# A decoder trunk in one kernel: earlier key loads, later output stores, and deeper query buffers in the last stage

## The chip, the core and the metric

The kernel runs on one core of a Trainium2 chip. Its engines are TensorE (PE, matrix products and transposes), VectorE (DVE), ScalarE (ACT), GpSimd (POOL), and SyncE (SP), whose queue issues the transfers (DMAs) between the chip's main memory and the on-chip buffer. Each engine works through its own list of instructions in the order in which they were put at build time; between engines they wait on semaphores. The metric is the device time of one execution in microseconds (us), the median over runs.

## The reference

One sequence of 2048 rows of width 1024, all in float32, goes through two layers:

```
layer A:  h = rms_norm(x)*(1+scale)+shift;  u,v,z = split(h @ w_in)
          y = gelu(u) * (causal_128x128_mix(rms_norm(gelu(v))) + b) * silu(z)
          x = x + gate * (y @ w_out)
keys:     k,v = split(rms_mod(x) @ w_kv);   k = rms_norm(k)    (3 groups x 2 heads of 128)
layer B:  q,z = split(rms_mod(x) @ w_in);   q = rms_norm(q)/sqrt(128)   (3 groups x 8 heads)
          for group g with dilation d in (1, 4, 16):
              each block of 128 (dilated) rows looks at its own and the previous block
              s = q k^T - slope*distance;  m = max s;  p = exp(s-m);  l = sum p
              o_g = p v / l;   lse_g = m + log l
          o = sum_g softmax_g(lse) * o_g;   out = x + gate * ((o * silu(z)) @ w_out)
```

The modulation (scale, shift, gate) comes from small products of a conditioning vector.

## The kernel before, in words

The 2048 rows are 16 tiles of 128, in four quarters. Each quarter passes through layer A, the key and value product, and the query and `z` products (`dense_s`, line 306, products of sums of blocks: `pd_z3ba` and its like); weights are loaded as `raw_*`, split in two halves by ACT (L260) and DVE (L262), and the matmuls are done in threes, as high x high, low x high and high x low. Queries, keys, `z` and attention outputs travel through main memory (`qd`, `kvd`, `zd`, `od`).

Attention works in units (g, b, kh): group, block of 128 queries, one of two key heads with its four query heads. A unit has four steps, of which a different one is done at each turn of `attend`. `att_1` takes the key block `kv` and the query block `qt` from main memory, transposes both on PE (`pk` L1362, `pq` L1374) and copies them back (`kT`, and `qT` by ACT L1379 and DVE L1380). `att_2` computes the scores (`ps` L1407 to L1409, twelve matmuls 128x256), adds the distance bias on DVE (L1413), takes the maximum (L1416, L1417) and the exponential on ACT (L1423). `att_3` transposes the weights (`pp` L1465, copied to `pT`), `att_4` multiplies with the values (`po` L1484), and stores `ot` to `od` (L1491). Four units are under way at once. The query of the next unit, and with the first of two heads its keys, are loaded in one go ahead of `att_1`. `qt` has two buffers, `kv` four (the tag `xin`), and eight buffers with the tag `st`, made by `sum_tile`, hold sums in the query and `z` products.

`attend` is a generator, run a step at a time between the matmuls of other stages: `tick` counts matmul groups and runs the generators in `fillers` at the rate `rate[0]`. Group 2 of all blocks runs beside the last quarter's products. Groups 1 and 0 of a quarter run as a filler of the following work (`attend_local`); for the last quarter this is the last stage, the output projection. For each tile t and half n of 512 columns it loads the residual rows (`xr`, L1666), issues the stores that were put off (`flush`, at L1667), runs 24 matmuls (`pf`, L1678 to L1680, with `wo`, and the transposed rows `yb` made by `make_yb`, L1638 to L1641), prepares tile t+2 from the three groups' outputs `og` and `z` (`prepare`: ACT L1613, DVE L1541, L1617, L1618), adds the residual (`of`, L1685) and puts its store off to the next `flush`.

What sets the order: the code runs once at build time, and a scheduler then puts each engine's instructions in a fixed order of its own from what depends on what, so that a change in one place can reorder others. Nearly all DMAs of the kernel are issued on SP, in order. Eight semaphores serve them in turn, so that a DMA on SP also waits for the landing of the eighth DMA before it.

Of the kernel before, what the change touches and what calls it, by code (L numbers as in the profile page):

```python
# [12 lines left out]
F32 = mybir.dt.float32  # L13
# [5 lines left out]
P = 128  # L19
# [3 lines left out]
NQ = 4  # L23
# [11 lines left out]
def trunk(ctx, tc, out, x, c, a_ada_w, a_ada_b, a_norm_g, a_w_in, a_sgu_g, a_w_spatial,  # L35
          a_b_spatial, a_w_out, kv_ada_w, kv_ada_b, kv_norm_g, w_kv, k_norm_g, b_ada_w,
          b_ada_b, b_norm_g, b_w_in, b_q_norm_g, b_w_out, dbg=None):
    nc = tc.nc
# [13 lines left out]
    bp = ctx.enter_context(tc.tile_pool(name="bp", bufs=2))  # L52
    sp = ctx.enter_context(tc.tile_pool(name="sp", bufs=4))
    tp = ctx.enter_context(tc.tile_pool(name="tp", bufs=8))
    ap_ = ctx.enter_context(tc.tile_pool(name="ap", bufs=2))
# [6 lines left out]
    od = [dp.tile([S, D], F32, name=f"od{g}") for g in range(3)]  # L62
# [14 lines left out]
    def fill(n):  # L77

        for _ in range(n):
            if not fillers:  # L80
                return
            g = fillers.pop(0)
            try:
                next(g)
                fillers.append(g)
            except StopIteration:
                pass
# [3 lines left out]
    def tick(part=1.0):  # L91
        rate[1] += rate[0] * part
        n = int(rate[1])
        rate[1] -= n
        fill(n)

    def drain():
        while fillers:
            fill(1)

    def evt(name, dt=F32):
        return ep.tile([P, 512], dt, tag="ev", name=name)

    def pst(name, tag="a"):
        return ps.tile([P, 512], F32, tag=tag, name=name)
# [145 lines left out]
    def flush():  # L251
        jobs = pending[:]
        pending.clear()
        with tc.issue_after(last_ld[0].ins):
            for out_, src in jobs:
                nc.sync.dma_start(out_, src)
# [252 lines left out]
    def sum_tile(nm):  # L509
        return tp.tile([P, 516], F32, tag="st", name=f"st_{nm}")  # L510
# [792 lines left out]
    def blk_rows(t, g, b):  # L1303

        if g == 0:
            return t[b * P:(b + 1) * P]
        if g == 1:
            n, r = divmod(b, 4)
            v = t.rearrange("(n i r) w -> n r i w", n=4, r=4) if len(t.shape) == 2 else \
                t.rearrange("(n i r) g w -> n r i g w", n=4, r=4)  # L1310
            return v[n, r]
        v = t.rearrange("(i r) w -> r i w", r=16) if len(t.shape) == 2 else \
            t.rearrange("(i r) g w -> r i g w", r=16)
        return v[b]
# [8 lines left out]
    def geom(g, b):  # L1323
        prev = None if g == 2 or (g == 0 and b == 0) or (g == 1 and b < 4) else b - (1, 4)[g]
        nk = 1 if prev is None else 2
        return prev, nk, 4 // nk

    def att_kv(g, b, ring):
        prev, nk, _ = geom(g, b)
        kv = xp.tile([P, 2, 512], F32, tag="xin", name=f"kv{g}_{b}")  # L1330
        if prev is not None:
            v, src = (t.rearrange("p (h two d) -> p h two d", h=2, two=2)
                      for t in (kv[:, 0, :], blk_rows(kvd, g, prev)[:, g, :]))
            if ring:
                nc.sync.dma_start(v[:, :, 1, :], src[:, :, 1, :])
            else:
                nc.sync.dma_start(v, src)
        nc.sync.dma_start(kv[:, nk - 1, :], blk_rows(kvd, g, b)[:, g, :])
        return kv.rearrange("p b (h two d) -> p b h two d", h=2, two=2)

    def att_q(g, b, kh):
        qt = ap_.tile([P, 516], F32, tag="qt", name=f"qt{g}_{b}_{kh}")
        nc.sync.dma_start(qt[:, 0:516], blk_rows(qd[g], g, b)[:, kh, 0:516])
        return qt

# [124 lines left out]
    def att_4(u):  # L1470

        g, b, kh = u["id"]
        _, nk, hp = geom(g, b)
        if g == 0:
            k4 = slice(kh * 4, kh * 4 + 4)
            l4 = slice(8 + kh * 4, 12 + kh * 4)
            e1, l1, l0 = stat[1][:, b, k4], stat[1][:, b, l4], stat[0][:, b, l4]
            scale_heads(nc.vector, u["o1"], u["o1"], e1)
            nc.vector.tensor_tensor(l1, l1, e1, ALU.mult)
            nc.vector.tensor_tensor(l0, l0, l1, ALU.add)  # L1480
        po = pst(f"po{g}_{b}_{kh}")
        for h in range(4):
            for j in range(nk):
                nc.tensor.matmul(po[:, h * P:(h + 1) * P], u["pT"][h // hp][:, h % hp, j, :],  # L1484
                                 u["kv"][:, j, kh, 1, :], start=j == 0, stop=j == nk - 1)
        ot = evt(f"ot{g}_{b}_{kh}")
        if g == 0:
            nc.vector.tensor_tensor(ot, po, u["o1"], ALU.add)
        else:
            evac_copy(ot, po)  # L1490
        nc.sync.dma_start(blk_rows(od[g], g, b)[:, kh * 512:(kh + 1) * 512], ot)  # L1491

    def attend_local(Q, wrap=False):

        bs = range(4 * Q, 4 * Q + 4)
        yield from attend([(1, b) for b in bs], wrap)
        v = stat[1][:, 4 * Q:4 * Q + 4, :]
        nc.sync.dma_start(std[1].rearrange("(n i r) c -> i n r c", n=4, r=4)[:, Q], v)
        yield
        nc.sync.dma_start(v, std[1].rearrange("(b i) c -> i b c", i=P)[:, 4 * Q:4 * Q + 4])  # L1500
        yield from attend([(0, b) for b in bs], wrap, 3)

    def attend(blocks, wrap=False, lead=0, skew=1):


        us = [{"id": (g, b, kh), "wrap": wrap and geom(g, b)[1] == 2}
              for g, b in blocks for kh in range(2)]
        for u in us:
            g, b, _ = u["id"]
            nk = geom(g, b)[1]  # L1510
            u["own"] = b % 2 if g == 0 and nk == 2 else nk - 1
            u["ring"] = g == 0 and nk == 2 and (0, b - 1) in blocks and geom(0, b - 1)[1] == 2

        def load(i):
            if i < len(us):
                g, b, kh = us[i]["id"]
                if kh == 0:
                    us[i]["kv"] = us[i + 1]["kv"] = att_kv(g, b, us[i]["ring"])
                us[i]["qt"] = att_q(g, b, kh)

        load(0)
        for _ in range(lead):
            yield
        for i in range(len(us) + 2 + skew):
            for k, st in ((2 + skew, att_4), (1 + skew, att_3), (1, att_2), (0, att_1)):
                if 0 <= i - k < len(us):
                    if k == 0:
                        load(i + 1)
                        if i % 2:
                            us[i]["kT"] = us[i - 1]["kT"]  # L1530
                        elif us[i]["ring"]:
                            us[i]["ring"] = us[i - 1]["kT"]
                    st(us[i - k])
                if i >= k:
                    yield


    def scale_heads(e, out, t, f):

        n = f.shape[-1]  # L1540
        e.tensor_tensor(out.rearrange("p (h d) -> p h d", d=P), t.rearrange("p (h d) -> p h d", d=P),  # L1541
                        f.unsqueeze(2).broadcast_to([P, n, P]), ALU.mult)
# [3 lines left out]
    def finish():  # L1546
# [80 lines left out]
            ys[0] = prepare(0, ogs[0])  # L1627

        def last():
            yield from attend_local(NQ - 1)  # L1630
            yield from weights(NT - TPQ, NT)

        def make_yb(t):
# [26 lines left out]
        for t in range(NT):  # L1660
            rw = slice(t * P, (t + 1) * P)
            yb = ybs[t]
            for n in range(2):
                ns = slice(n * 512, (n + 1) * 512)
                xr = evt(f"xr1{t}_{n}")
                last_ld[0] = nc.sync.dma_start(xr, x1d[rw, ns])  # L1666
                flush()  # L1667
                pt = pst(f"pf{t}_{n}", "d")
                wh, wl = wo[n]
                if n and t + 1 < NT:  # L1670
                    make_yb(t + 1)
                    if t + 3 == NT - TPQ:
                        drain()
                        ogs.update({i: load(i) for i in (t + 3, t + 4)})
                elif n == 0 and t + 4 < NT and t + 4 not in (NT - TPQ, NT - TPQ + 1):
                    ogs[t + 4] = load(t + 4)
                for k in range(KT):
                    nc.tensor.matmul(pt, yb[:, 0, k, :], wh[:, k, :], start=k == 0, stop=False)  # L1678
                    nc.tensor.matmul(pt, yb[:, 0, k, :], wl[:, k, :], start=False, stop=False)  # L1679
                    nc.tensor.matmul(pt, yb[:, 1, k, :], wh[:, k, :], start=False, stop=k == KT - 1)  # L1680
                    tick(0.125)
                    if k % 4 == 2 and t + 2 < NT:
                        ys[t + 2] = prepare(t + 2, ogs[t + 2], 2 * n + k // 4)
                o_ = evt(f"of{t}_{n}")
                nc.vector.tensor_tensor(o_, pt, xr, ALU.add)  # L1685
                pending.append((out[rw, ns], o_))

# [72 lines left out]
```

## Time and profile before

| | |
|---|---|
| median of 3 runs | 2903.24 us (2902.45 to 2907.31) |
| profiled execution | 2904.99 us, its span 2903.3 us |
| PE busy | 2875.6 us of the span |
| DVE, ACT, POOL busy | 2219.1, 1667.6, 258.2 us |
| mean granted clock of TensorE | 0.999 |
| DMA | 239 GB/s over the span |

A profile's busy time is an engine's own; "idle before" is the time in which it stood ahead of an instruction, with what ended that. The granted clock is given as a share of 2.4 GHz: 1.00 is 2.4, 0.50 is 1.2. A span is measured inside an execution, from its first instruction to its last; the execution's own time is some 1.7 us longer.

### The profile page before, as it was taken

What the parts mean: (1) busy time and instruction counts of PE and PEld (TensorE: products, weight loads), DVE (VectorE), ACT (ScalarE), POOL (GpSimd) and SP (SyncE); (2) the same over time, 40 slices, a digit from 0 to 9 for tenths busy, and PEclk for the clock granted to TensorE, in tenths of its full rate; (3) what the DMA queues carried; (4) which work ended last, traced back from release to release, by engine and by line L of the source; (5) the groups of instructions that cost most, each with busy time, mean ns of one, the idle gap of its engine ahead of it and who ended that gap; (6) DMA issues with size and microseconds to landing.
All of it is one profiled execution on the core that took longest, in us unless ns stands there. A gap on an engine that the chain in (4) does not pass through costs nothing. (4 is left out here: it accounts for less than half of the span.)

```text
span 2903.3 us, 44921 instructions
## 1 busy us (share of the span) xinstructions
PE 2875.6 (99%) x14610; PEld 2419.2 (83%) x14610; DVE 2219.1 (76%) x4246; ACT 1667.6 (57%) x3400; POOL 258.2 (9%) x549
## 2 busy tenths in 40 slices
PE   8999999999999999999999999999999999999999
PEld 5888888888888888888888888888888888988887
DVE  6786677787758986887878876987678876888972
ACT  4423345668456765676555665676355667876540
POOL 1000001101011000000010000000010003311100
PEclk9999999999999999999999999999999999999999
DMA  7899788777998577776676676766554667889842
GB/s 258 298 311 297 265 287 292 241 250 249 311 334 284 171 259 225 239 247 201 212 262 198 192 253 212 243 225 197 172 174 155 223 219 238 269 265 340 260 144 87
DMA packets 390783, 693.82 MB, mean 239 GB/s; under 512 B 42027, under 2 KB 119821, under 8 KB 390549
## 3 DMA queue, kind: packets, MB, share of 16 engines
q1 hardware_dynamic: 390548, 690.97, 72.3%
q8 instruction: 115, 1.88, 0.3%
q14 instruction: 120, 0.98, 0.1%
HBM read 530.97 MB, written 159.85 MB: 238 GB/s over the span
## 5 line engine op out<-in xcount | busy, mean ns | idle before, releaser
L306 PE MATMUL pd_kv<-w_kv,hkh 128*128 128x512 f32 x768 | 238.5, 391 | 0.3 <-DMA w_kv<-wk 0.2
L355 PE MATMUL pd_u<-hAh,w_u 128*128 128x512 f32 x512 | 207.8, 406 | 0.0
L355 PE MATMUL pd_z<-hAh,w_z 128*128 128x512 f32 x512 | 205.8, 402 | 0.0
L1423 ACT ACTIVATE pr<-pr,stat,rt 128x256 f32<-128x256 f32 (+1 forms) x320 | 177.4, 556 | 45.3 <-DVE stat L1420 30.0
L357 PE MATMUL pd_u<-hAh,w_u 128*128 128x512 f32 x512 | 200.6, 392 | 1.7 <-DVE w_u L262 1.7
L357 PE MATMUL pd_z<-hAh,w_z 128*128 128x512 f32 x512 | 200.4, 392 | 0.0
L356 PE MATMUL pd_u<-hAl,w_u 128*128 128x512 f32 x512 | 200.0, 391 | 0.0
L356 PE MATMUL pd_z<-hAl,w_z 128*128 128x512 f32 x512 | 199.8, 390 | 0.0
L306 PEld LDWEIGHTS pd_kv<-w_kv,hkh 128*128 128x128 f32 x768 | 143.3, 188 | 30.1 <-ACT w_kv L260 0.6
L1484 PEld LDWEIGHTS po<-kv,pT 128*128 128x128 f32 x1200 | 147.6, 191 | 7.4 <-ACT pT L1321 1.2
L1484 PE MATMUL po<-kv,pT 128*128 128x128 f32 x1200 | 149.8, 275 | 1.0 <-ACT pT L1321 1.0
L306 PE MATMUL pd_kv<-w_kv,hkl 128*128 128x512 f32 x384 | 149.8, 390 | 0.0
L1351 POOL TENSOR_SCALAR rt<-qt 128x4 f32<-128x4 f32 x96 | 26.8, 279 | 1311.9 <-DMA qt<-qd 724.7
L1413 DVE SCALAR_TENSOR_TENSOR pr<-dist,rt,ps 128x256 f32<-128x256 f32 (+1 forms) x320 | 124.7, 431 | 22.4 <-PE ps L1409 10.4
L260 ACT ACTIVATE w_u<-raw_u 128x512 fp32r<-128x512 f32 x96 | 59.5, 628 | 142.4 <-PE pd_u L357 95.2
L260 ACT ACTIVATE w_o<-raw_o 128x512 fp32r<-128x512 f32 x104 | 64.2, 628 | 96.4 <-PE pd_o L306 37.8
L260 ACT ACTIVATE w_q<-raw_q 128x512 fp32r<-128x512 f32 x144 | 88.6, 628 | 49.9 <-PE pd_kv L306 9.9
L357 PEld LDWEIGHTS pd_u<-hAh,w_u 128*128 128x128 f32 x512 | 96.1, 188 | 23.9 <-DVE w_u L262 2.9
L357 PEld LDWEIGHTS pd_z<-hAh,w_z 128*128 128x128 f32 x512 | 96.1, 188 | 21.0
L355 PEld LDWEIGHTS pd_u<-hAh,w_u 128*128 128x128 f32 x512 | 96.5, 188 | 18.4 <-issue 1.7
L356 PEld LDWEIGHTS pd_z<-hAl,w_z 128*128 128x128 f32 x512 | 96.5, 188 | 17.6
L355 PEld LDWEIGHTS pd_z<-hAh,w_z 128*128 128x128 f32 x512 | 96.4, 188 | 17.4
(866 smaller groups left out, 7944.8 us busy)
## 6 DMA issues: line engine op xcount, KB each, us to landing
raw_q<-in_b_w_in_dram SPq DMA_DIRECT2D x144, 256.0 KB, 3.8
w_z<-wuz SPq DMA_DIRECT2D x64, 512.0 KB, 4.3
raw_o<-in_a_w_out_dram SPq DMA_DIRECT2D x104, 256.0 KB, 3.5
qt<-qd SPq DMA_DIRECT2D x96, 258.0 KB, 3.6
raw_v<-in_a_w_in_dram SPq DMA_DIRECT2D x96, 256.0 KB, 4.0
raw_u<-in_a_w_in_dram SPq DMA_DIRECT2D x96, 256.0 KB, 5.3
od<-ot SPq DMA_DIRECT2D x96, 256.0 KB, 2.5
raw_kv<-in_w_kv_dram SPq DMA_DIRECT2D x76, 256.0 KB, 4.7
```

The costliest lines, as they stand in the source:

```text
L260: nc.scalar.activation(hi, src, AF.Copy)
L306: last_mm[0] = nc.tensor.matmul(pt, a, u[:, w, :], start=f, stop=e, skip_group_check=more)
L355: nc.tensor.matmul(pts[i], wh, hh[:, k, :], start=k == 0, stop=False)
L356: nc.tensor.matmul(pts[i], wh, hl[:, k, :], start=False, stop=False)
L357: nc.tensor.matmul(pts[i], wl, hh[:, k, :], start=False, stop=k == KT - 1)
L1351: nc.gpsimd.tensor_scalar(rt[:, 12:16], u["qt"][:, 512:516], 1.0 / P, EPS, ALU.mult, ALU.add)
L1413: nc.vector.scalar_tensor_tensor(pr[:, i, :], dist3[:, d0:d0 + w], u["rt"][:, h:h + 1], psc[:, i, :], ALU.mult, ALU.add)
L1423: nc.scalar.activation(pr[:, i, :], pr[:, i, :], AF.Exp, bias=mneg[:, i:i + 1], scale=u["rt"][:, h:h + 1], accum_out=lsum[:, i:i + 1])
L1484: nc.tensor.matmul(po[:, h * P:(h + 1) * P], u["pT"][h // hp][:, h % hp, j, :], u["kv"][:, j, kh, 1, :], start=j == 0, stop=j == nk - 1)
```

## The change

Three parts. In all attention, the loads of keys and queries are apart: keys are loaded a unit ahead of before, and the stores of `ot`, kept in the list `stores`, are issued at the start of the next step in place of the end of their own. With `deep=True`, which only the last quarter's `attend_local` sets, `qt` is taken from the eight `st` buffers (`sum_tile`), and loaded two units ahead. In the last stage, `flush` stands behind the fourth of eight matmul triples (k == 3) rather than ahead of the first, and `of` goes to the two buffers of the tag `bc`.

```diff
--- before.py
+++ after.py
@@ -1338,8 +1338,9 @@
         nc.sync.dma_start(kv[:, nk - 1, :], blk_rows(kvd, g, b)[:, g, :])
         return kv.rearrange("p b (h two d) -> p b h two d", h=2, two=2)
 
-    def att_q(g, b, kh):
-        qt = ap_.tile([P, 516], F32, tag="qt", name=f"qt{g}_{b}_{kh}")
+    def att_q(g, b, kh, deep):
+        nm = f"qt{g}_{b}_{kh}"
+        qt = sum_tile(nm) if deep else ap_.tile([P, 516], F32, tag="qt", name=nm)
         nc.sync.dma_start(qt[:, 0:516], blk_rows(qd[g], g, b)[:, kh, 0:516])
         return qt
 
@@ -1488,22 +1489,23 @@
             nc.vector.tensor_tensor(ot, po, u["o1"], ALU.add)
         else:
             evac_copy(ot, po)
-        nc.sync.dma_start(blk_rows(od[g], g, b)[:, kh * 512:(kh + 1) * 512], ot)
-
-    def attend_local(Q, wrap=False):
+        u["stores"].append((blk_rows(od[g], g, b)[:, kh * 512:(kh + 1) * 512], ot))
+
+    def attend_local(Q, wrap=False, deep=False):
 
         bs = range(4 * Q, 4 * Q + 4)
-        yield from attend([(1, b) for b in bs], wrap)
+        yield from attend([(1, b) for b in bs], wrap, deep=deep)
         v = stat[1][:, 4 * Q:4 * Q + 4, :]
         nc.sync.dma_start(std[1].rearrange("(n i r) c -> i n r c", n=4, r=4)[:, Q], v)
         yield
         nc.sync.dma_start(v, std[1].rearrange("(b i) c -> i b c", i=P)[:, 4 * Q:4 * Q + 4])
-        yield from attend([(0, b) for b in bs], wrap, 3)
-
-    def attend(blocks, wrap=False, lead=0, skew=1):
-
-
-        us = [{"id": (g, b, kh), "wrap": wrap and geom(g, b)[1] == 2}
+        yield from attend([(0, b) for b in bs], wrap, 3, deep=deep)
+
+    def attend(blocks, wrap=False, lead=0, skew=1, deep=False):
+
+
+        stores = []
+        us = [{"id": (g, b, kh), "wrap": wrap and geom(g, b)[1] == 2, "stores": stores}
               for g, b in blocks for kh in range(2)]
         for u in us:
             g, b, _ = u["id"]
@@ -1511,21 +1513,34 @@
             u["own"] = b % 2 if g == 0 and nk == 2 else nk - 1
             u["ring"] = g == 0 and nk == 2 and (0, b - 1) in blocks and geom(0, b - 1)[1] == 2
 
-        def load(i):
+        def load_kv(i):
             if i < len(us):
-                g, b, kh = us[i]["id"]
-                if kh == 0:
-                    us[i]["kv"] = us[i + 1]["kv"] = att_kv(g, b, us[i]["ring"])
-                us[i]["qt"] = att_q(g, b, kh)
-
-        load(0)
+                g, b, _ = us[i]["id"]
+                us[i]["kv"] = us[i + 1]["kv"] = att_kv(g, b, us[i]["ring"])
+
+        def load_q(i):
+            if i < len(us):
+                us[i]["qt"] = att_q(*us[i]["id"], deep)
+
+        def store():
+            for dst, t in stores:
+                nc.sync.dma_start(dst, t)
+            stores.clear()
+
+        load_kv(0)
+        load_q(0)
+        if deep:
+            load_q(1)
         for _ in range(lead):
             yield
         for i in range(len(us) + 2 + skew):
             for k, st in ((2 + skew, att_4), (1 + skew, att_3), (1, att_2), (0, att_1)):
                 if 0 <= i - k < len(us):
+                    store()
                     if k == 0:
-                        load(i + 1)
+                        load_q(i + 1 + deep)
+                        if i % 2 == skew - 1:
+                            load_kv(i + 3 - skew)
                         if i % 2:
                             us[i]["kT"] = us[i - 1]["kT"]
                         elif us[i]["ring"]:
@@ -1533,6 +1548,7 @@
                     st(us[i - k])
                 if i >= k:
                     yield
+        store()
 
 
     def scale_heads(e, out, t, f):
@@ -1627,7 +1643,7 @@
             ys[0] = prepare(0, ogs[0])
 
         def last():
-            yield from attend_local(NQ - 1)
+            yield from attend_local(NQ - 1, deep=True)
             yield from weights(NT - TPQ, NT)
 
         def make_yb(t):
@@ -1664,7 +1680,6 @@
                 ns = slice(n * 512, (n + 1) * 512)
                 xr = evt(f"xr1{t}_{n}")
                 last_ld[0] = nc.sync.dma_start(xr, x1d[rw, ns])
-                flush()
                 pt = pst(f"pf{t}_{n}", "d")
                 wh, wl = wo[n]
                 if n and t + 1 < NT:
@@ -1679,9 +1694,11 @@
                     nc.tensor.matmul(pt, yb[:, 0, k, :], wl[:, k, :], start=False, stop=False)
                     nc.tensor.matmul(pt, yb[:, 1, k, :], wh[:, k, :], start=False, stop=k == KT - 1)
                     tick(0.125)
+                    if k == 3:
+                        flush()
                     if k % 4 == 2 and t + 2 < NT:
                         ys[t + 2] = prepare(t + 2, ogs[t + 2], 2 * n + k // 4)
-                o_ = evt(f"of{t}_{n}")
+                o_ = bp.tile([P, 512], F32, tag="bc", name=f"of{t}_{n}")
                 nc.vector.tensor_tensor(o_, pt, xr, ALU.add)
                 pending.append((out[rw, ns], o_))
 
```

The work on each engine stays as it was. What moves on PE is the last stage, above all its start. Ahead of this piece stand, in both kernels, the last `pd_z3bb` products, `pyb0`, `pk1_12` and two `pf0_0`. Here is PE of before, from the transposes of the query of unit (1,12,0) on (`pq1_12_0`); `pf0_0` and `pf0_1` are the two halves of tile 0 of the output projection, `ps1_12_00` the unit's first scores:

```order
L1374 MATMUL pq1_12_0_26328<-ident_136,qt1_12_0_26311 128x128
L1680 MATMUL pf0_0_26296<-wo00_25081,yb0_26233 128x512
L1374 MATMUL pq1_12_0_26328<-ident_136,qt1_12_0_26311 128x128 x3
L1678 MATMUL pf0_0_26296<-wo00_25081,yb0_26233 128x512
L1679 MATMUL pf0_0_26296<-wo01_25086,yb0_26233 128x512
L1680 MATMUL pf0_0_26296<-wo00_25081,yb0_26233 128x512
L1678 MATMUL pf0_0_26296<-wo00_25081,yb0_26233 128x512
L1679 MATMUL pf0_0_26296<-wo01_25086,yb0_26233 128x512
L1680 MATMUL pf0_0_26296<-wo00_25081,yb0_26233 128x512
L306 MATMUL pd_z3ba0_25841<-w_z3b22_0_26187,hob33_21805 128x512
L306 MATMUL pd_z3ba1_25842<-w_z3b22_0_26187,hob33_21805 128x512
L1407 MATMUL ps1_12_00_26342<-kT1_12_26325,qT1_12_0_26333 128x256
```

In the changed kernel the same transposes stand at the end of all of tile 0's matmuls and of the products `pd_z3ba`, and the scores right behind them:

```order
L1693 MATMUL pf0_1_26458<-wo10_25997,yb0_26233 128x512
L1694 MATMUL pf0_1_26458<-wo11_26122,yb0_26233 128x512
L1695 MATMUL pf0_1_26458<-wo10_25997,yb0_26233 128x512
L1375 MATMUL pq1_12_0_26331<-ident_136,st_qt1_12_0_26309 128x128 x4
L1408 MATMUL ps1_12_00_26345<-kT1_12_26328,qT1_12_0_26336 128x256
L1409 MATMUL ps1_12_00_26345<-kT1_12_26328,qT1_12_0_26336 128x256
L1408 MATMUL ps1_12_01_26359<-kT1_12_26328,qT1_12_0_26336 128x256
L1409 MATMUL ps1_12_01_26359<-kT1_12_26328,qT1_12_0_26336 128x256
L1410 MATMUL ps1_12_00_26345<-kT1_12_26328,qT1_12_0_26336 128x256
L1408 MATMUL ps1_12_00_26345<-kT1_12_26328,qT1_12_0_26336 128x256
L1409 MATMUL ps1_12_00_26345<-kT1_12_26328,qT1_12_0_26336 128x256
L1410 MATMUL ps1_12_00_26345<-kT1_12_26328,qT1_12_0_26336 128x256
```

Between `pq1_12_0` and its scores no other matmul is left. Somewhat later on PE, before, the weights' transposes of the unit (`pp1_12_00`, `pp1_12_01`) stand among the last matmuls of `pf0_1`:

```order
L1678 MATMUL pf0_1_26457<-wo10_25997,yb0_26233 128x512
L1465 MATMUL pp1_12_00_26399<-ident_136,pr1_12_00_26343 128x128 x2
L1679 MATMUL pf0_1_26457<-wo11_26122,yb0_26233 128x512
L1680 MATMUL pf0_1_26457<-wo10_25997,yb0_26233 128x512
L1465 MATMUL pp1_12_00_26399<-ident_136,pr1_12_00_26343 128x128 x2
L1678 MATMUL pf0_1_26457<-wo10_25997,yb0_26233 128x512
L1679 MATMUL pf0_1_26457<-wo11_26122,yb0_26233 128x512
L1465 MATMUL pp1_12_01_26406<-ident_136,pr1_12_01_26357 128x128 x2
L1407 MATMUL ps1_12_10_26424<-kT1_12_26325,qT1_12_1_26390 128x256
L1408 MATMUL ps1_12_10_26424<-kT1_12_26325,qT1_12_1_26390 128x256
L1465 MATMUL pp1_12_01_26406<-ident_136,pr1_12_01_26357 128x128 x2
```

In the changed kernel the same transposes come right behind the unit's scores and the next query's transposes, and are followed by that query's scores:

```order
L1375 MATMUL pq1_12_1_26385<-ident_136,st_qt1_12_1_26311 128x128 x4
L1466 MATMUL pp1_12_00_26401<-ident_136,pr1_12_00_26346 128x128 x4
L1466 MATMUL pp1_12_01_26408<-ident_136,pr1_12_01_26360 128x128 x2
L1408 MATMUL ps1_12_10_26426<-kT1_12_26328,qT1_12_1_26390 128x256
L1466 MATMUL pp1_12_01_26408<-ident_136,pr1_12_01_26360 128x128 x2
L1409 MATMUL ps1_12_10_26426<-kT1_12_26328,qT1_12_1_26390 128x256
```

All `pf0_1` matmuls have been done by then. On SP, before, the loads of these two queries stand among weights of the third quarter's query product (`raw_q30t4`):

```order
L267 DMA raw_q30t4_0_25734<-wt0_3_106 128x512
L1343 DMA qt1_12_0_26311<-qd1_93 128x516
L267 DMA raw_q30t4_1_25739<-wt0_3_106 128x512
L267 DMA raw_q30t4_2_25744<-wt0_3_106 128x512
L1491 DMA od2_97<-ot2_13_1_25495 128x512
L1343 DMA qt1_12_1_26313<-qd1_93 128x516
```

In the changed kernel they stand behind the loads for tiles 3 and 4 of the output projection:

```order
L1614 DMA og3_0_26284<-od0_95 128x1024
L1614 DMA og3_2_26286<-od2_97 128x1024
L1621 DMA zt3_0_26288<-zd_101 128x512
L1621 DMA zt3_1_26289<-zd_101 128x512
L1682 DMA xr10_0_26292<-x1d_90 128x512
L1614 DMA og4_0_26295<-od0_95 128x1024
L1614 DMA og4_2_26297<-od2_97 128x1024
L1621 DMA zt4_0_26299<-zd_101 128x512
L1621 DMA zt4_1_26300<-zd_101 128x512
L1344 DMA st_qt1_12_0_26309<-qd1_93 128x516
L1344 DMA st_qt1_12_1_26311<-qd1_93 128x516
L1344 DMA st_qt1_13_0_26313<-qd1_93 128x516
```

They have moved by some eighty rows on SP, and are now the first of four queries in a row (the fourth is `qt1_13_1`). The keys of this block, `kv1_12`, stand well ahead of them in both kernels.

## Rows read from the trace of the kernel before

**Rows 1.** The page's first part: busy us of each engine, share of the span, instructions.

```profile
PE 2875.6 (99%) x14610; PEld 2419.2 (83%) x14610; DVE 2219.1 (76%) x4246; ACT 1667.6 (57%) x3400; POOL 258.2 (9%) x549
```

**Rows 2.** PE's waits: engine, line <- what ended the wait: us in all, times, longest.

```profile
PE pva L126 <- DMA veca<-in_a_ada_b_dram: 5.0, 1, 5.0
...
PE pd_o1a L306 <- DVE w_o L262: 1.8, 2, 1.6
PE pd_u L357 <- DVE w_u L262: 1.7, 2, 1.0
PE pp L1465 <- ACT pr L1423: 1.6, 1, 1.6
PE pf L1680 <- DVE yb L1641: 1.4, 1, 1.4
...
PE pd_v10a L306 <- DVE w_v L262: 1.0, 2, 0.8
```

**Rows 3.** Waits of SP's DMA queue, same columns.

```profile
SPq L1343 <- PE pq L1374: 137.9, 67, 6.9
...
SPq L256 <- DVE of L1685: 95.0, 28, 5.5
```

**Rows 4.** PE's timeline, start of last stage: start us, us, line, what, shape, count.

```profile
2619.28 5.61 PE L306 MATMUL pd_z3bb<-w_z3bt,hob 128*128 128x512 f32 x24
...
2626.80 0.27 PE L1374 MATMUL pq<-ident,qt 128*128 128x128 f32 x1
...
2630.41 5.18 PE L306 MATMUL pd_z3ba<-w_z3b,hob 128*128 128x512 f32 x22
...
2644.47 0.38 PE L1465 MATMUL pp<-ident,pr 128*128 128x128 f32 x2
...
2651.77 0.50 PE L1680 MATMUL pf<-wo,yb 128*128 128x512 f32 x1 [1.41 <-DVE yb L1641]
```

**Rows 5.** SP's timeline: DMA issues around the last stage's start.

```profile
2557.89 0.32 SPq L1343 DMA_DIRECT2D qt<-qd  x1
...
2633.58 1.00 SPq L1598 DMA_DIRECT2D og<-od  x2
2634.92 0.99 SPq L1605 DMA_DIRECT2D zt<-zd  x2
...
2644.05 0.32 SPq L1343 DMA_DIRECT2D qt<-qd  x1
```

**Rows 6.** DMA issues from 2620 to 2655 us: count, KB each, median us to landing.

```profile
og<-od SPq DMA_DIRECT2D x9, 512.0 KB, 6.3
zt<-zd SPq DMA_DIRECT2D x8, 256.0 KB, 7.7
...
qt<-qd SPq DMA_DIRECT2D x3, 258.0 KB, 3.2
```

**Rows 7.** ACT's timeline, first unit of group 1.

```profile
2627.67 0.69 ACT L1379 ACTIVATE qT<-pq,gqk 128x512 fp32r<-128x512 f32 x1
...
2642.24 1.28 ACT L1423 ACT_TABLE_LOAD   x1 [1.55 <-DVE stat L1417]
2643.53 0.60 ACT L1423 ACTIVATE pr<-pr,stat,rt 128x256 f32<-128x256 f32 x1
```

**Rows 8.** DVE's timeline, the same unit.

```profile
2628.39 0.75 DVE L1380 SCALAR_TENSOR_TENSOR qT<-pq,gqk,qT 128x512 fp32r<-128x512 f32 x1
...
2639.85 1.26 DVE L1413 SCALAR_TENSOR_TENSOR pr<-dist,rt,ps 128x256 f32<-128x256 f32 x3
...
2642.01 0.15 DVE L1417 SCALAR_TENSOR_TENSOR stat<-rt 128x2 f32<-128x2 f32 x1
```

**Rows 9.** Stretches: us, busy us (count) of PE, PEld, DVE, ACT, POOL, granted clock, DMA, GB/s.

```profile
22.00:24.00 2.00, 1.91 (x3) 0.87 (x4) 1.93 (x4) 0.30 (x1) 0.00 (x0) 0.50 1.05 368
26.00:28.00 2.00, 2.00 (x4) 0.73 (x4) 1.88 (x3) 0.00 (x0) 0.00 (x0) 0.66 1.10 349
2650.00:2652.00 2.00, 0.59 (x3) 0.24 (x2) 2.00 (x5) 2.00 (x8) 1.20 (x2) 1.00 0.34 123
```

## Prediction

> **What bounds the kernel now.** I read the page's busy shares first: TensorE (PE) is busy 2875.6 us, 99% of the span [rows 1]. So a microsecond that any other engine, or a transfer, saves is worth nothing unless PE waits for it, and a microsecond in which PE newly waits goes to the end in full: nothing later has slack to win it back. The second view was the list of PE's waits. With a span of 2903.3 us, PE idles 27.7 us in all. The largest item is the start, before any work (5.0 us for the first vector), and the waits in the body are few and small: 1.8 us for `w_o`, 1.7 for `w_u`, 1.6 for the softmax (`pp`), 1.4 for `yb`, 1.0 for `w_v` [rows 2]. No PE wait in this list is put down to `qt`, `kv`, `od` or `xr`, the transfers that the change moves. They are held up on SP's queue, it is true: the query loads stood 137.9 us behind the last use of their buffer, the output stores 95.0 us behind their sum [rows 3]. But these are waits of a queue that PE doesn't feel. So there is little to win, at most 7.5 us of the body's waits in rows 2, and only as far as late loads cause them. What matters is whether the new order lays bare something that PE's other work covers today.
>
> The third view was PE's timeline where the last stage begins. There unit (1,12,0), the first of the last quarter's group 1, passes through PE beside tile 0 of the output projection. Its `pq` transposes stand at 2626.80, and the first `pp`, which needs its softmax, at 2644.47; the 17.7 us between hold 22 matmuls `pd_z3ba` in a row (5.18 us) and nearly all of tile 0's `pf` [rows 4]. ScalarE (ACT), VectorE (DVE) and this unit's chain have all that time. Its query was asked for at 2557.89, 69 us before use [rows 5].
>
> **The change, part by part.** Keys a unit earlier, stores a step later: the count of loads, stores and arithmetic is the same. On PE the order of the first 7,260 rows or so (everything before the last stage) is unchanged. What can move there is when a weight arrives, behind fewer held issues on SP. The waits of that kind are 1.8 + 1.7 + 1.0 = 4.5 us [rows 2]; they end with DVE's half of the weight split, which has other reasons to be late than SP. I take a third of them, −1.5 us. Bounds: −5 (all of them, and a little more), and +2 (a key load moved in front of a weight makes another wait of the size of the longest in rows 2).
>
> Deep query buffers: the load of `qt1_12_0` goes from among the `raw_q30t4` weights to a place behind `og3`, `zt3`, `xr10_0`, `og4` and `zt4`. SP issues in order, and a DMA goes out only when the eighth before it has landed: `qt1_13_0` at 2644.05 is the eighth behind the second `zt3` issue, about 2635.5, so 8.5 us later, though nothing in its own data held it [rows 5]. The new eighth before `qt1_12_0` is `og3_2`, issued about 2634.3 [rows 5]. An `og` load took 6.3 us here, a `zt` load 7.7, a `qt` load at the end of this busy stretch 3.2 [rows 6]. So the query is issued between 2640.6 and 2642.8, and lands after another 3.2 to 8.5: between 2643.8 and 2651.3. The stretch is full of half-megabyte loads, so I take issue at 2642.1 and 7.0 us, 2649.1.
>
> When does PE want it? In the new order 70 matmuls 128x512 (24 of `pd_z3ba`, of which 22 are the row at 2630.41, and tile 0's 48 `pf`, less the two that stand ahead of `pq` in both) come before `pq1_12_0`. One costs at most 5.61/24 = 0.23 us [rows 4], so 16.1, and PE is there at 2626.80 + 16.1 = 2642.9. Term A, the wait for the query: 2649.1 − 2642.9 = 6.2 us, bounds 0.9 and 8.4. In before it is 0.
>
> Term B, the bare softmax chain. In the new order `pq`, twelve scores, the second `pq`, and the `pp` of the same unit follow each other with no other matmul between. From the landing: `pq` 0.6 (two `pp` transposes took 0.38 [rows 4], four under twice that); `qT` on ACT then DVE, 2627.67 to 2629.14, 1.5 [rows 7, 8]; twelve scores of half a 512 width, 1.4, of which some 0.5 lie beside DVE's part; DVE's bias, maximum and statistics 2639.85 to 2642.16, 2.3 [rows 8]; a table load of 1.28 that starts only when the statistics are there, and four exponentials of 0.6 [rows 7]. Together 0.6 + 1.5 + 0.9 + 2.3 + 1.3 + 2.4 = 9.0 until the last `pp` can start. PE's own work within is 0.6 + 1.4 + 0.6 + 0.5 = 3.1. That would leave 5.9; DVE starts on the first scores before the last are there, so I take 5.5, bounds 4.2 (the table load is out of the way) and 6.5 (`of0_1`, which waits for its late `xr`, now stands between the two statistics on DVE).
>
> Term C: `pf` waited 1.4 us for `yb` in tile 1 [rows 2, 4]. Less work stands between `ps1_12_1` and its `pp` now (four `pf` in place of fourteen), and `yb` has the same two copies ahead, so I change one wait against another of its size: 0, bounds −1.4 and +1.5. Rows from mid tile and `of` in the `bc` buffers touch SP and DVE only: 0, hidden by the `pf` matmuls; without that cover one 128x512 sum, no more than 0.7.
>
> Term D: the clock. With A and B, PE does about 3 us of work in some 15. Early in the kernel, behind the small products of its start, the granted clock was 0.50 at 22 to 24 us (1.2 GHz in place of 2.4), and 0.66 over 26 to 28, on its way back; after the 1.4 us wait for `yb` it was still 1.00 [rows 9]. If the clock falls here it costs as there: 22 to 26 at 0.5 loses 2.0 us and 26 to 28 another 0.7, 2.7 us. The Trainium skill, "TensorE: Matmul & The Clock Gate", Part 1 (The HAM clock gate), says it the other way round: "the default state is throttled, and activity releases the throttle", a rule that speaks against any order with a bare wait. The slow stretch of rows 9 agrees with it; no run here shows yet what a 6 us wait in the body does. By the rule D is 2.7, without it 0. I take 2.7, since two long waits lie close together; bounds 0 and 5.4, if it falls twice.
>
> **Sum.** A 6.2 + B 5.5 + C 0 + D 2.7 − 1.5 = +12.9 us. The profiled execution took 2904.99 us (span 2903.3 and 1.7 around it), 1.75 above the median of the runs, 2903.24. So 2904.99 + 12.9 = 2917.9 for one like it, and 2916.1 for the median. All low ends together give 0.9 + 4.2 − 1.4 + 0 − 5 = −1.3, 2901.9; all high ends 8.4 + 6.5 + 1.5 + 5.4 + 2 = +23.8, 2927.0.
>
> **The rivals.** *The clock holds.* A and B come as above, D is 0: +10.2, 2913.4. For it: the 1.00 after a 1.4 us wait. Against: that wait was a quarter of A.
>
> *The query arrives in time.* SP, no longer behind the `zd` stores and `pq` releases, issues `og3` and `og4` sooner and the query lands as fast as the 3.2 us row: A 0.9, B 4.2, D 0, C 0, −1.5: +3.6, 2906.8, within the noise. For it: SP's queue does lose its long holds [rows 3]. Against: the eighth-DMA rule of rows 5 is not about such holds, and the stretch moves as many bytes as before.
>
> *Faster.* The relief on SP decides: from the point where weights, `yb` and `pp` inputs arrive a microsecond or two sooner throughout, the 7.5 us of rows 2 in the body go, with some 3 us of smaller ones like them, while the query comes in time (A 0) and B is 4.2: −6.3, 2896.9. Against: PE's order leaves B bare whatever SP does, and those waits end with DVE or ACT, none with a load.
>
> *Worse.* Each of the next units stands as bare as the first, since the fillers were spent on tile 0. A second wait of B's size and a longer slow clock: 12.9 + 5.5 + 1.5 = +19.9, 2923.1. For it: `pp1_12_1` has only four `pf` ahead. Against: from the third unit on, `pf` matmuls stand between the steps again.
>
> **How the numbers follow.** Forecast with the clock low 0.40, clock holds 0.27, in time 0.16, faster 0.08, worse 0.09. The range 2903 to 2922 leaves out about 0.10 below and 0.09 above. The likeliest case alone, with its bounds narrowed to one wait of each kind, is 2911 to 2921. About 0.2% (5.8 us) is what a measurement of this kernel can tell from no change: faster than 2897.4 has 0.08, slower than 2909.0 has the first two, the worst, and a little less for their low ends: 0.75; between them 0.17.
>
> **What would show it.** In the profile after: a PE wait at `pq` for the DMA `qt` of 5 to 8 us, near the 16th us of the last stage; right behind it waits at `ps` for `qT` and at `pp` for `pr` that sum to 4 to 6.5; a granted clock near 0.5 in some of the next 5 us; and up to there a PE timeline within 2 us of before. The prediction is wrong if PE's idle time in the last stage doesn't grow by more than 5 us, or if PE's waits for the weights fall by more than 4.

## The result, and the profile after

The changed kernel took 2924.14 us in the median of six runs (2920.27 to 2928.05), the kernel before 2906.72 beside it: a ratio of 1.0065, 95% interval 1.0052 to 1.0078, or 15 to 23 us slower. A second timing on another chip (experiment e6) gave 1.0059 (1.0047 to 1.0071). The forecast was +12.9 us, 2916.1, with a range up to 2922: the right sign and the right place, too small a loss. Of the miss of 8 us, 3.5 is the three runs of before on which it stood, whose median was 2903.24. Four executions of the experiments below took 4,858 to 11,926 us and are left out of the ratios; the traces of e7 and e14 are of two of them and are not used.

The page of the changed kernel, its first part, and its list of PE's waits (cut to what differs; columns as in [rows 1] and [rows 2]):

```profile
PE 2882.4 (99%) x14610; PEld 2423.4 (83%) x14610; DVE 2221.7 (76%) x4246; ACT 1669.1 (57%) x3400; POOL 261.0 (9%) x549
```
```profile
PE pq L1375 <- DMA st_qt<-qd: 5.7, 1, 5.7
...
PE pp L1466 <- ACT pr L1424: 4.4, 4, 2.8
PE pd_u L355 <- ACT w_u L260: 2.2, 1, 2.2
...
PE pq L1375 <- DVE pr L1414: 1.7, 1, 1.7
```

In a span of 2920.5 us PE idles 38.1, in place of 27.7, and is busy for 6.8 us more with the same instructions. The largest new wait is the forecast one, `pq` for the query, 5.7 us; the longest wait of `pp`, 2.8 us, and one of 0.8 at `ps` belong to the bare softmax chain; the wait for `yb` of [rows 2] is gone. A wait of `pd_u` for ACT's copy of a weight, 2.2 us, was not forecast.

PE's timeline in the last stage answers to [rows 4] (start, us, line, what, count):

```profile
2631.23 5.17 PE L306 MATMUL pd_z3ba<-w_z3b,hob 128*128 128x512 f32 x22
...
2644.40 0.39 PE L1695 MATMUL pf<-wo,yb 128*128 128x512 f32 x1
2650.51 1.09 PE L1375 MATMUL pq<-ident,st_qt 128*128 128x128 f32 x4 [5.72 <-DMA st_qt<-qd]
2652.38 0.58 PE L1408 MATMUL ps<-kT,qT 128*128 128x256 f32 x1 [0.78 <-ACT qT L1380]
...
2659.00 1.85 PE L1466 MATMUL pp<-ident,pr 128*128 128x128 f32 x6 [2.84 <-ACT pr L1424]
...
2660.86 0.63 PE L1466 MATMUL pp<-ident,pr 128*128 128x128 f32 x2
...
2664.91 0.60 PE L1363 MATMUL pk<-ident,kv 128*128 128x128 f32 x4
```

The 22 `pd_z3ba` are there as before; then `pf` runs without a break, the last from 2644.40; then PE stands for the query until 2650.51, for `qT`, and for `pr`. The two kernels' way over the same work, from the first `pyb0` to `pk1_13`, before and after, and stretches of the changed kernel (columns as in [rows 9]; the sixth number behind the engines is the granted clock):

```profile
2624.73:2648.83 24.10, 23.84 (x134) 20.00 (x133) 19.95 (x37) 18.44 (x45) 0.00 (x0) 1.00 1.04 401
```
```profile
2626.07:2664.91 38.84, 29.20 (x133) 23.96 (x132) 30.02 (x52) 23.74 (x63) 8.58 (x16) 0.78 1.04 400
2646.00:2648.00 2.00, 0.00 (x0) 0.00 (x0) 2.00 (x4) 0.83 (x3) 0.00 (x0) 0.84 1.03 393
2648.00:2656.00 8.00, 4.71 (x20) 4.10 (x20) 6.52 (x13) 2.30 (x7) 4.85 (x8) 0.50 1.05 402
2656.00:2664.00 8.00, 5.16 (x23) 4.42 (x23) 5.01 (x12) 7.23 (x19) 3.74 (x8) 0.50 1.04 397
2664.00:2666.00 2.00, 2.00 (x15) 1.86 (x14) 2.00 (x6) 1.33 (x3) 0.00 (x0) 0.89 0.85 322
```

24.10 us have become 38.84, 14.7 more: 9.4 of idle time, and 5.4 because the same matmuls run at half clock from 2647 to 2664. Of the span's 17.2 us, 1.3 lie ahead of this stretch and 1.1 behind it.

SP's timeline answers to [rows 5]:

```profile
2634.39 1.00 SPq L1614 DMA_DIRECT2D og<-od  x2
2635.96 1.00 SPq L1621 DMA_DIRECT2D zt<-zd  x2
2637.87 0.32 SPq L1682 DMA_DIRECT2D xr<-x1d  x1
2639.20 0.99 SPq L1614 DMA_DIRECT2D og<-od  x2
2640.55 2.47 SPq L1621 DMA_DIRECT2D zt<-zd  x2
2643.77 2.34 SPq L1344 DMA_DIRECT2D st_qt<-qd  x4
```

The first of the four queries goes out at 2643.77, some 8.7 us behind the `og` that is its eighth before (the second of the pair of 2634.39, sent at 2635.1). It was used 6.7 us later. The forecast said 2642.1 and 7.0 us, in a trace that came to this place 1.3 us sooner.

### The profile page after: what moved, and what is told of

It reads as the page before. It is cut to its first block, busy times and chain, and to the rows that moved or that the text cites. A ratio compares the mean times of both kernels' runs of the same rounds, so it can differ in the third digit from the quotient of the medians.

```text
span 2920.5 us, 44920 instructions
## 1 busy us (share of the span) xinstructions
PE 2882.4 (99%) x14610; PEld 2423.4 (83%) x14610; DVE 2221.7 (76%) x4246; ACT 1669.1 (57%) x3400; POOL 261.0 (9%) x549
## 5 line engine op out<-in xcount | busy, mean ns | idle before, releaser
L260 ACT ACTIVATE w_u<-raw_u 128x512 fp32r<-128x512 f32 x96 | 59.7, 628 | 139.9 <-PE pd_u L357 92.1
L260 ACT ACTIVATE w_o<-raw_o 128x512 fp32r<-128x512 f32 x104 | 64.3, 628 | 95.2 <-PE pd_o L306 37.6
L260 ACT ACTIVATE w_q<-raw_q 128x512 fp32r<-128x512 f32 x144 | 88.9, 628 | 50.9 <-PE pd_kv L306 9.9
L355 PEld LDWEIGHTS pd_z<-hAh,w_z 128*128 128x128 f32 x512 | 96.4, 188 | 17.4
```

The lines of the kernel that those rows point to most:

```text
L260: nc.scalar.activation(hi, src, AF.Copy)
L355: nc.tensor.matmul(pts[i], wh, hh[:, k, :], start=k == 0, stop=False)
```

## The experiments

Theory 1 was the forecast's: the late place of the first query's load, brought by the deep buffers, is the loss. All ratios are against the kernel before on the same chip, with a 95% interval.

**e1, keys and stores.** Edit to the changed kernel (this and the next three; `...` marks lines left out, and the `flush()` put in stands ahead of the tile's matmuls, as before):

```diff
-            yield from attend_local(NQ - 1, deep=True)
+            yield from attend_local(NQ - 1)
...
+                flush()
...
-                    if k == 3:
-                        flush()
...
-                o_ = bp.tile([P, 512], F32, tag="bc", name=f"of{t}_{n}")
+                o_ = evt(f"of{t}_{n}")
```

> Only the keys a unit earlier and the stores a step later; query buffers and last stage as before. Theory 1 (the loss is the late place of the first query's load, which the deep buffers bring): the query stands where it stood, PE order of the last stage as before, so no wait at pq above 0.5 us, no slow clock, and 0 to +2 us against before (the changed kernel's PE came 1.3 us later to the last stage; if that is the keys' and stores' doing it shows here as +1 to +2). Rival (the moved keys and stores crowd the queue at the stage's start): a wait of 3 us or more at pq and +10 us or more.

Measured: 1.0012 (1.0004 to 1.0021), +3.5 us. There is no wait at `pq`. The clock is at half only from 2631 to 2634, behind a wait of 2.1 us for a weight (`w_z3b`), shown in the last section. Not the last stage's loss, but a loss: the first sign that the keys' or stores' term had the wrong sign.

**e2, all but the last stage's part** (the last five edited lines of that diff alone).

> The changed kernel without the last stage's part (stores at the tile's start, output rows in the old buffers); deep query buffers kept. Theory 1: the whole loss is here, pq waits 5 to 7 us for its query, the clock is at half for 14 to 18 us, +15 to +19 us against before. Rival (residual rows running ahead in the queue make the query late): without them the query lands 3 us or more sooner, and the loss is at most +9 us.

Measured: 1.0049 (1.0037 to 1.0061), +14.2 us, a little under the forecast 15 to 19. The wait at `pq` is there without the residual rows running ahead, and longer:

```profile
PE pq L1375 <- DMA st_qt<-qd: 7.7, 1, 7.7
```

The rival falls: deep buffers alone make the query late.

**e3, the first two queries in the old buffers.**

```diff
-                us[i]["qt"] = att_q(*us[i]["id"], deep)
+                us[i]["qt"] = att_q(*us[i]["id"], deep and (us[i]["id"][0] == 0 or i > 1))
```

> The changed kernel, but the first two queries of the last quarter's group 1 are taken from the two old query buffers; the other fourteen stay deep. Theory 1: the first load goes out some 80 us before its use again, pq stands among tile 0's matmuls, no long wait, clock full; -1 to +3 us against before, that is 14 to 18 us less than the changed kernel. Rival (deep buffers cost by their number of transfers in flight, wherever the first stands): at least half of the loss stays, +8 us or more.

Measured: 1.0014 (1.0005 to 1.0022), +4.1 us, about what e1 has without any deep buffer, and 1 us above the forecast since the keys' loss stays in it. PE's order at the stage's start is that of before, and `pq` and `pp` stand 17.4 us apart with matmuls between:

```profile
2630.64 0.27 PE L1375 MATMUL pq<-ident,qt 128*128 128x128 f32 x1
...
2648.00 0.38 PE L1466 MATMUL pp<-ident,pr 128*128 128x128 f32 x2
```

The first query is sent at 2561.73, 69 us ahead of its use, as before. Theory 1 holds: the other fourteen deep queries cost nothing that this can tell, the first two 14 us (1.0062, the mean of the changed kernel's two timings, less 1.0014).

**e4, no deep buffers** (the first two lines of e1's diff alone).

> The changed kernel without the deep query buffers: keys, stores and the last stage's part stay. Theory 1: -1 to +2 us against before, with PE waits of the last stage as before (1.4 us for yb or less). Rival (stores at mid tile and residual rows far ahead cost by themselves): +5 us or more, in waits of the last stage.

Measured: 1.0013 (1.0005 to 1.0022), +3.8 us: neither forecast, but equal to e1. Stores at mid tile and `of` in `bc` add nothing that these times can tell.

**e5, the wait filled with work.** 24 matmuls more, which the build puts between tile 0's last `pf` and `pq`; their result is not read:

```diff
+                if t == 0 and n == 1:
+                    dum = pst("dummy", "d")
+                    for i in range(24):
+                        nc.tensor.matmul(dum, yb[:, 0, i % KT, :], wh[:, i % KT, :], start=i == 0, stop=i == 24 - 1)
```

> The changed kernel with 24 matmuls 128x512 more, whose result nobody reads, between tile 0's last matmul and pq, in the wait for the query (5.4 us of work at full clock in a wait of 5.7). Theory of the clock (the fall to half, from 2647 to 2664 us, costs as much as the waits' remainder suggests): granted clock 1.00 through pq and the scores, the way from pyb0 to pk1_13 shorter by 3 to 5 us than the changed kernel's 38.8, and about +13 to +15 us against before, for 24 matmuls more of work. Rival (the slow clock only fills time in which PE would wait for ACT and DVE anyway): the way is 38 to 40 us and the time that of the changed kernel, or more.

Measured: 1.0061 (1.0049 to 1.0073), the time of e6. PE's timeline and stretches of it:

```profile
2621.89 1.03 PE L1654 MATMUL pyb<-ident,og 128*128 128x128 f32 x8
...
2640.39 5.60 PE L1704 MATMUL dummy<-wo,yb 128*128 128x512 f32 x24
2646.05 0.63 PE L1375 MATMUL pq<-ident,st_qt 128*128 128x128 f32 x4
2647.45 0.39 PE L1408 MATMUL ps<-kT,qT 128*128 128x256 f32 x1 [0.78 <-ACT qT L1380]
...
2654.27 1.86 PE L1466 MATMUL pp<-ident,pr 128*128 128x128 f32 x6 [3.81 <-ACT pr L1424]
...
2660.36 0.60 PE L1363 MATMUL pk<-ident,kv 128*128 128x128 f32 x4
```
```profile
2645.00:2650.00 5.00, 3.54 (x23) 2.63 (x22) 3.93 (x8) 0.83 (x2) 3.59 (x5) 1.00 1.05 401
2652.00:2654.00 2.00, 0.00 (x0) 0.00 (x0) 2.00 (x6) 1.76 (x2) 1.41 (x3) 0.82 1.01 391
2654.00:2658.00 4.00, 3.73 (x16) 3.14 (x17) 1.26 (x3) 4.00 (x15) 1.78 (x3) 0.50 1.05 388
2658.00:2660.00 2.00, 2.00 (x12) 2.00 (x11) 1.66 (x5) 0.79 (x3) 0.35 (x2) 0.50 1.02 405
```

`pq` and the scores now run at full clock (four `pq` in 0.63 us, not 1.09). The wait of `pp` has grown from 2.84 to 3.81 us and the clock falls there instead. From the first `pyb0` to `pk1_13` it is 38.5 us (2621.89 to 2660.36) against 38.8 in the changed kernel, though the clock is at half for some 7 us in place of 17. The theory of 3 to 5 us falls, the rival holds: up to `pp` the slow clock filled time in which PE waits for DVE and ACT anyway. What it does cost is behind `pp`, where PE has its work ready: from the last two `pp` (2660.86) to `pk1_13` 4.05 us in the changed kernel, where the like stretch of before, with one `pf` more, took 2.5:

```profile
2646.30 0.38 PE L1465 MATMUL pp<-ident,pr 128*128 128x128 f32 x2
...
2648.83 0.60 PE L1362 MATMUL pk<-ident,kv 128*128 128x128 f32 x4
```

In e5 the clock is at half in this part too; no run has it at full clock behind a bare chain.

**e6, the changed kernel again,** unedited.

> The changed kernel once more, to stand beside the others on this chip. From its first timing: +15 to +22 us against before (ratio 1.0052 to 1.0078), a wait of 5 to 8 us at pq, clock at half for some 17 us.

Measured: 1.0059 (1.0047 to 1.0071), a wait of 6.0 us at `pq`.

**e7 and e8, stores alone and keys alone.** Both on e1's kernel; e7 takes back the keys (first diff, and two lines that do nothing without `deep`), e8 the stores (second diff):

```diff
-                        load_q(i + 1 + deep)
-                        if i % 2 == skew - 1:
-                            load_kv(i + 3 - skew)
+                        if i % 2:
+                            load_kv(i + 1)
+                        load_q(i + 1)
```

```diff
-        u["stores"].append((blk_rows(od[g], g, b)[:, kh * 512:(kh + 1) * 512], ot))
+        nc.sync.dma_start(blk_rows(od[g], g, b)[:, kh * 512:(kh + 1) * 512], ot)
```

> Only the stores a step later, keys and all else as before. Theory (the +3.5 us of keys and stores together come from the keys, whose loads make a weight of the second quarter late, seen as a wait of 1 to 3 us at pd_u near 786 us): 0 to +1 us against before, no wait there above 1 us. Rival (the stores do it): +2.5 to +4 us.

> Only the keys a unit earlier, stores and all else as before. Theory: +2.5 to +4 us, with the wait at pd_u near 786 us of 1 to 3 us. Rival (the stores do it): 0 to +1 us and no such wait.

Measured: stores 0.9999 (0.9990 to 1.0007), keys 1.0013 (1.0004 to 1.0021), +3.8 us. The keys do it.

**e9 and e10, the keys by stage.** In e8's kernel the early place is made conditional on the block: `blocks[0][1] < NT - TPQ` for e9, `>=` for e10, groups 0 and 1 in both.

> Keys a unit earlier in the first three quarters' attention alone (groups 1 and 0 beside the other layers), the last stage as before, stores as before; on PE the order is that of before, on SP 42 loads and stores change places. Theory (the 3.8 us of the keys lie where the second quarter's weights wait, near 786 us): +2.5 to +4 us. Rival (they lie in the last stage, where the keys' change alone alters PE's order): 0 to +1 us.

> Keys a unit earlier in the last stage alone; everything up to it as before. Theory: 0 to +1 us. Rival: +2.5 to +4 us, seen in waits of PE behind the 2650th us.

Measured: 1.0013 (1.0004 to 1.0022) and 1.0002 (0.9994 to 1.0011). So the loss lies ahead of the last stage, though the two intervals overlap. In e9 PE's order is that of before to its last instruction.

**e11 and e12, two traces:** the kernel before, and e7's.

> The kernel before, for a second trace. If the wait near 786 us for the weight of pd_u comes from the keys, it is absent or below 1 us here, as in the first trace; if it comes and goes by itself, it may be here too.

> Only the stores a step later, for a trace. By the timing (ratio 0.9999) it should read like before: no wait above 1 us near 786 us, PE order the same, span within 4 us of 2903.

Measured: 2908.14 and 2906.17 us, one run each; no wait near 786 us in either. In e12's trace the order on every engine is that of before until the 2667th us, where SP's first differs: later stores moved nothing ahead of the last stage.

**e13, e14, e15, the keys by quarter.** The condition is `blocks[0] == (1, 0)`, `blocks[0] == (0, 0)`, and the second and third quarters.

> Keys a unit earlier only in the first quarter's group 1 (beside layer A of the second quarter, 600 to 800 us); here raw_u136 falls behind an output store on SP, and w_u142 behind the exponentials and two table loads on ACT. Theory (the keys' loss is the wait of pd_u for w_u142 near 786 us): +2 to +4 us, with that wait of 0.3 to 3 us. Rival (the loss is spread over all the moved loads): at most +1.5 us, and the rest in the two runs beside this one.

> Keys a unit earlier only in the first quarter's group 0. Theory: 0 to +1 us and no wait near 786 us. Rival: +1 to +2 us.

> Keys a unit earlier only in the second and third quarters' attention. Theory: 0 to +1 us, no wait near 786 us. Rival: +1 to +2 us.

Measured: 1.0011 (1.0002 to 1.0020), 1.0003 (0.9994 to 1.0012), 1.0003 (0.9994 to 1.0011). The first quarter's group 1 has 3.2 of the keys' 3.8 us; the other two can't be told from none. The intervals overlap, so the times alone don't part the three, but the traces do. PE's longest wait between 780 and 792 us in e13:

```profile
PE pd_u L355 <- ACT w_u L260: 2.3, 1, 2.3
```

This wait stands in all ten traces of kernels that have this group's keys early (0.2 to 3.2 us, 1.8 in the mean) and in none of the six without. What the place costs PE can be read between two `pd_u` matmuls that stand 19 matmuls apart in every kernel, before and after:

```profile
786.16 0.39 PE L356 MATMUL pd_u<-hAl,w_u 128*128 128x512 f32 x1
...
790.05 0.39 PE L356 MATMUL pd_u<-hAl,w_u 128*128 128x512 f32 x1
```
```profile
785.43 0.39 PE L356 MATMUL pd_u<-hAl,w_u 128*128 128x512 f32 x1
...
788.26 0.50 PE L355 MATMUL pd_u<-hAh,w_u 128*128 128x512 f32 x1 [2.20 <-ACT w_u L260]
...
792.34 0.39 PE L356 MATMUL pd_u<-hAl,w_u 128*128 128x512 f32 x1
```

That is 3.89 us before and 6.91 after. In the ten traces it is longer than before by 1.1 to 6.8 us, 3.2 in the mean; in the other five without early keys, to within 0.01 us, it is the same. So this one place makes most of the keys' 3.8 us. The largest three (e2 6.8, e3 5.7, e6 4.2) are those in which the clock falls there too; in e2:

```profile
790.00:792.00 2.00, 1.52 (x3) 0.79 (x4) 2.00 (x4) 1.18 (x3) 0.00 (x0) 0.50 0.98 375
```

Two things move there. On SP, before and after, from 764 us on:

```profile
763.82 0.43 SPq L342 DMA_DIRECT2D raw_u<-in_a_w_in_dram  x1
766.47 0.33 SPq L1491 DMA_DIRECT2D od<-ot  x1
...
775.55 0.46 SPq L342 DMA_DIRECT2D raw_u<-in_a_w_in_dram  x1
```
```profile
766.45 0.33 SPq L1527 DMA_DIRECT2D od<-ot  x1
...
769.27 0.98 SPq L342 DMA_DIRECT2D raw_u<-in_a_w_in_dram  x2
...
776.15 1.36 SPq L342 DMA_DIRECT2D raw_u<-in_a_w_in_dram  x1
```

A weight load, `raw_u136` by the built order, went out at 763.82, ahead of an output store that waits for its `ot` until 766.47. Now it stands behind that store and goes out at 769.27. But this is not the weight that PE waits for: `w_u142` comes two loads later, and its load goes out at 775.55 before and 776.15 after (the fiftieth of `raw_u` in both), 0.6 us apart. What is late is its copy on ACT:

```profile
782.06 0.63 ACT L260 ACTIVATE w_u<-raw_u 128x512 fp32r<-128x512 f32 x1 [2.76 <-DMA raw_u<-in_a_w_in_dram]
782.71 1.28 ACT L1423 ACT_TABLE_LOAD   x1
```
```profile
781.97 1.28 ACT L1424 ACT_TABLE_LOAD   x1 [3.40 <-DVE stat L1418]
...
785.31 1.28 ACT L1047 ACT_TABLE_LOAD   x1
...
787.57 0.63 ACT L260 ACTIVATE w_u<-raw_u 128x512 fp32r<-128x512 f32 x1
```

Before, the copy of `w_u142` (L260 at 782.06) comes ahead of a table load, four exponentials and another table load with two more functions. After, it stands behind them all, at 787.57, and PE waits for it until 788.26. PE waits for no key load here: moving the keys moved one weight's load on SP and another weight's copy on ACT in the built order, and the second is what PE feels. Whether the first brought about the second is not shown.

**e16, repaired:** e3's edit and the keys as before (e7's diff, with `load_q(i + 1 + deep)`).

> The changed kernel with both losses taken out: the first two queries of the last quarter's group 1 in the two old buffers, and the keys loaded where they were; stores later, the other queries deep, rows at mid tile stay. If the two account for all of the change's loss: -2 to +1 us against before. Rival (the deep queries and the last stage's part cost or give something of their own that the two losses hid): outside that, on either side.

Measured: 1.0009 (1.0000 to 1.0018), +2.6 us at 2900.55 to 2916.79. The two losses make some 15 of 18 us (1.0062 less 1.0009); whether the rest of the change has a small price of its own stays open, since the interval begins at none. No version that beats the kernel before shows itself: stores alone and the last stage's keys are level with it.

## Why the prediction was wrong

*What bounds the kernel* held: PE's new idle time and its slower matmuls are the whole difference. The stores' 95.0 us and the queries' 137.9 us behind others [rows 3] are 86.7 and 111.3 in the changed kernel, and PE had nothing of it.

*Term A*, 6.2 us: 5.7 in the profile, 6.0 in e6, 7.7 in e2. The order on SP and the rule of the eighth DMA gave it.

*Terms B and D*, 5.5 + 2.7 = 8.2: the stretch's 14.7 less A leaves 9.0. But the split was wrong in kind. Idle time beside A was 3.7 us, under B's lower bound of 4.2, and longer matmuls made 5.4, D's upper bound. From the use of the query to the last `pp` it took 10.4 us (2650.51 to 2660.86), 9.0 forecast; the slow clock's longer matmuls are mostly inside waits, as e5 showed, and not a price beside them, as term D had it. A + B + D were 14.4, measured 14.7: that it came so near is in part luck.

The Trainium skill's "TensorE: Matmul & The Clock Gate", Part 1 (The HAM clock gate), says that activity releases the throttle. The trace agrees: the clock falls from 1.00 to 0.50 in the wait for the query, near 2647, and is back near 2664, when PE has been at work again. What the fall costs was decided here by what else PE waited for.

*Term C*, 0, bounds −1.4 and +1.5: the 1.4 us for `yb` went, 1.7 us for `pq` behind DVE came late in the stage, and the work behind `pk1_13` took 1.1 us more. This is within its bounds; the residual rows and `of` were level, as taken (e4 against e1).

*The step that failed* is the first term, keys a unit earlier and stores a step later, which should have given a gain: "I take a third of them, −1.5 us. Bounds: −5 [...] and +2". The runs show a loss of 3.8 (e8, 1.2 to 6.1), all of it from the keys (e7). The list of waits in [rows 2] named the waits that could shrink, and I counted the SP holds as the reason that could be taken away. What the change did was to put the copy of one weight behind the exponentials on ACT, so that PE passes the place near 786 us later by 3.2 us in the mean of ten traces. The upper bound of +2 named a late weight, but too small and on SP alone. The move was in the built order of ACT, SP and DVE, where PE's order was unchanged, and I read only PE's for the first 7,260 rows. With +3.8 in place of −1.5 the sum is 18.2, between the two timings' +17.1 (0.59% of 2903.8) and +18.9 (0.65% of 2906.7). The rest of the miss is, to about a microsecond, the 3.5 us of the base.

*Chances*: of the rivals, "in time" and "faster" fell with A; "the clock holds" fell in the trace; "worse" named the right total (+19.9) by a mechanism that isn't there: the next units were not bare (behind `pk1_13` no wait of PE is longer than 1.7 us).

The changed kernel's own trace has 3.0 us of loss near 786 us, and yet PE comes to the last stage only 1.3 us late. Single executions differ by as much elsewhere: the kernel before, traced again in e11, comes to this place 1.9 us later than in its first trace. That is why the cost is read from one matmul to another, and not from the start.

## What to carry to other kernels

A deeper buffer taken from another stage's pool can make the first loads later: here the first went out behind the other stage's work, 6.7 us ahead of its use in place of 69, and what had been covered lay bare. Why the build put it there is not shown; that it goes back with the old buffers is (e3). Keep the old buffers for the first units and deepen from the third. And where the order on the bounding engine doesn't change, compare the order on the engines that feed it all the same: the price here was a weight's copy on ACT that slid behind exponentials.

## What was not expected of the hardware

Twenty-four more matmuls of 512 columns, 5.6 us of PE time, put into a wait cost nothing that can be told (1.0061 against 1.0059), and a full clock through them gained nothing either. The granted clock, once at half, stayed there while PE was busy again: 0.50 over 2656 to 2664, where PE worked 5.2 of 8 us, and 0.89 in the two microseconds after.

Nor does the length of a wait alone tell whether the clock falls. In e1 a wait of 2.06 us at the last stage's start brought it to half; the changed kernel's wait of 2.20 us near 786 us left it at 1.00, and e2's of 3.2 us at the same place did not. Here is e1:

```profile
2630.62 1.12 PE L306 MATMUL pd_z3ba<-w_z3b,hob 128*128 128x512 f32 x2 [2.06 <-ACT w_z3b L260]
```
```profile
2632.00:2634.00 2.00, 2.00 (x8) 1.71 (x8) 1.28 (x2) 0.55 (x1) 0.00 (x0) 0.50 1.03 396
```
